# First feed-forward matrix by halves of its input for two blocks at once, two modulation groups wholly on VectorE

## The chip, the core and the metric

The kernel runs on one core of a Trainium2 chip. The metric is the device time of one execution in microseconds (us). Short names: PE is TensorE's matrix multiplication, PEld its weight loads, DVE is VectorE, ACT is ScalarE, POOL is GpSimd, SP is SyncE, whose queue issues most of the loads.

## The reference, cut to what matters

One encoder layer over 256 tokens of width 2048: windowed attention, then a squared-ReLU feed-forward part of width 8192, each between a modulation by the condition c and a layer norm.

```python
c_act = silu(c)
sh_m, sc_m, g_m, sh_f, sc_f, g_f = split(c_act @ mod_w + mod_b, 6)   # mod_w: 2048 x 12288
y = windowed_gqa_sink(x * (1 + sc_m) + sh_m, ...)                    # 32 heads, 8 key heads
x = layer_norm(ALPHA * x + (1 + g_m) * y, ln_mix_g, ln_mix_b)
hff = x * (1 + sc_f) + sh_f                                          # 256 x 2048
u = square(relu(hff @ w1 + b1))                                      # w1: 2048 x 8192
y = u @ w2 + b2                                                      # w2: 8192 x 2048
x = layer_norm(ALPHA * x + (1 + g_f) * y, ln_mlp_g, ln_mlp_b)
```

## The kernel before

**Arithmetic.** Every large product is made of three: each operand is split into a high part (rounded to the 32-bit matmul format) and a low part (the rest), and high x high, high x low and low x high are summed in PSUM. The high part of a weight piece is cast on ACT (line 218, `wh`), the low part subtracted on DVE (line 190, `wl`).

**The stream.** All weights come in pieces of 1 MB (128 x 2048) through one ordered list, `S.q`, filled by `S.plan` before any work is emitted. Five raw buffers (`RAWS`) take the loads from SP's queue, in the order of the list. `pump` walks along the list: a weight piece gets its two casts and its two low parts when there is room (five half pieces of each kind); a *modulation step* (a piece with a `use`) is carried out there and then, at most two for each call. `S.main()` hands out the next weight piece, `S.done()` returns half of it and pumps. At `S.stop`, the end of the attention part, the walk halts until the feed-forward part begins; `S.vecs(4)` then carries out the four steps that are planned behind it.

**Modulation.** `Mod` computes c_act @ (columns of mod_w). `m_mix` and `m_ff` are scale and shift of the two parts in groups of columns; a group of `m_ff` belongs to 4 of the 16 input tiles of hff and has 8 steps, 2 input tiles each. A step listed in the group's `dve` is two accumulating instructions of 128 x 1024 on DVE (lines 304 and 306), any other is 8 narrow matmuls on PE (line 274), which the profile records as 16. If a group has DVE steps, a closing matmul quad (8 records) adds the accumulator's rows up. `ff_columns(g)` then turns the result into per-input scale and bias by transposes (line 326) and small DVE work; `ff_input(g)` transposes four tiles of the normed rows `xs` (line 834), applies scale and bias, and splits the result (lines 840 to 848) into `h2[g]`. `m_gm` and `m_gf` are the gates, 16 steps each; `m_gf` is wholly on DVE.

**Attention slots.** Slots n = -2 to 20 interleave the score, softmax and value work of 16 head groups with late `wqkv` pieces and, from n = 5, the 16 pieces of `wo` (`project`). `SLOT_FILL` says how many modulation steps are planned ahead of each slot's piece: 34 in all, that is `m_gm`, groups 0 and 1 of `m_ff` and two steps of group 2; four more stand behind the stop. Slots 3 and 4 have no weight piece. In the last call of `project` the residual is added, the statistics are taken (`add_gated`, `norm_scalars`, lines 688 to 704) and the first quarter of `xs` is normed (`normed`, lines 717 and 719).

**Feed-forward.** Four blocks of 16 hidden tiles of 128. Block 0's first matrix goes by halves of the input: `W1A` lists the pieces `w1a[kg, fq]` (4 input tiles x 4 hidden tiles), first for input tiles 0 to 7 (kg 0 and 1) and then for 8 to 15; three 256-wide matmuls for each pair of tiles (lines 904 to 906). After the first half ACT copies the sums into `uacc` (line 910), after the second DVE adds them (line 912), and `square_split` makes the hidden rows. `W1_FILL` plans the remaining steps of groups 2 and 3 between the pieces. Blocks 1 to 3 use `ff_hidden`: pieces `w1b`, one hidden tile and all 16 input tiles each, with a 512-wide and a 256-wide matmul for each pair (lines 928 and 929). `ff_out` is the second matrix, 16 pieces a block (lines 439 to 441). The steps of `m_gf` lie beside block 1. `xs` stays in its four buffers from the first norm to the end; in block 1 it is prepared for the last residual (lines 973 and 974). All 128 x 1024 work tiles come from one pool of 26 buffers (`g4`).

**Order.** The text of the program gives the priority of an instruction on its engine; the tile framework places one that it reckons ready ahead of earlier ones that are not, and adds the waits.

Of the kernel before, what the change touches and what calls it, by code (L numbers as in the profile page):

```python
# [11 lines left out]
F32 = mybir.dt.float32  # L12
# [8 lines left out]
S = 256  # L21
# [20 lines left out]
def hybrid_kernel(ctx: ExitStack, tc: tile.TileContext, a, out: bass.AP):  # L42
# [6 lines left out]
    gen = ctx.enter_context(tc.tile_pool(name="gen", bufs=26))  # L49
    psa = ctx.enter_context(tc.tile_pool(name="psa", bufs=5, space=PSUM))  # L50
# [310 lines left out]
    m_ff = groups(a["modf"], FFG, [(1, 5, 7), (1, 4, 5, 6), (2,), (1, 2, 4, 5, 6, 7)])  # L361
# [30 lines left out]
    late = [m_gm] + [m[0] for m in m_ff[:3]]  # L392
# [9 lines left out]
    W1_FILL = [1, 1, 1, 0, 0, 2, 0, 3, 0, 0, 0, 0, 0, 0, 0, 0]  # L402
    SLOT_FILL = dict(enumerate([0, 1, 2, 1, 0, 1, 3, 0, 1, 3, 2, 0, 3, 5, 1, 1, 3, 2, 1, 3, 0, 0, 1], -2))
# [9 lines left out]
    W1A = [(kg, fq) for p in ((0, 1), (2, 3)) for q in ((0, 1), (2, 3)) for kg in p for fq in q]  # L413
    for n, (kg, fq) in enumerate(W1A):
        left = [m.n - m.planned for m, _, _ in m_ff]
        for _ in range(max(W1_FILL[n], left[2] if n == 6 else 0, left[2] + left[3] if n == 8 else 0)):
            m_ff[2 if m_ff[2][0].planned < m_ff[2][0].n else 3][0].plan()
        S.plan(a["w1a"][kg, fq])
    NF = FF // 128 // BLK
    for blk in range(BLK):  # L420
        for f in range(NF):
            if blk:
                if blk == 1 and f % 2:
                    m_gf.plan()
                S.plan(a["w1b"][(blk - 1) * NF + f])
        for c in range(4):
            for kg in range(4):
                if blk == 1 and kg % 2:
                    m_gf.plan()
                S.plan(a["w2"][blk, c, kg], None, blk == BLK - 1 and c == 3 and kg > 1)  # L430
# [423 lines left out]

    h2 = [ff_input(0)]
    for c in range(1, 4):
        for t in range(NT):
            normed(c, t)

# [25 lines left out]
    uacc = [g4() for _ in range(4)]  # L885
    us = []
    opened = {}
    for n, (kg, fq) in enumerate(W1A):
        if n in (1, 7, 9):
            ff_columns(len(h2))  # L890
            h2.append(ff_input(len(h2)))
        wh, wl = S.main()
        for fp in range(2):
            if kg % 2 == 0:
                opened[fq, fp] = psa.tile([128, 512], F32, name="pa")
# [61 lines left out]
    for blk in range(BLK - 1):  # L957
        if blk:
            us = ff_hidden(blk)
# [133 lines left out]
```

## Time and profile before

| | |
|---|---|
| median of 3 runs | 1133.12 us (1132.92 to 1133.7) |
| profiled execution | 1131.72 us |
| span of its instructions | 1130.0 us |
| mean granted PE clock | 0.994 |
| moved | 288.50 MB, mean 255 GB/s |

The attention part lasts until about 388.6 us of the span, the feed-forward part from there to 1117.4, and the last norm and stores follow. In rows of groups, "busy" is the union of a group's durations and the last number is the idle time of the engine ahead of them; matmuls are pipelined, so the time of one in a sequence is read from start to start, not from its length.

### The profile page before, as it was taken

The numbers are of one execution on the slowest core, as the hardware profiler recorded it, in microseconds if no ns is written. First come the engines' busy times: TensorE is split into PE (matmuls) and PEld (weight loads), VectorE is DVE, ScalarE is ACT, GpSimd is POOL, SyncE is SP. The second block draws the span as 40 slices with busy tenths as digits, with TensorE's granted clock in tenths as the row PEclk, the third lists the DMA queues.
The fourth block names the chain that finished last, engine by engine and source line by source line (L and its number), as shares of the span: only waits on it lengthen the run. The fifth ranks groups of instructions, "written<-read, shape, count | busy, mean of one in ns | idle before, by whom it ended". The sixth has DMA issues, their size and how long they took to land.

```text
span 1130.0 us, 15722 instructions
## 1 busy us (share of the span) xinstructions
PE 1091.6 (97%) x6224; PEld 876.6 (78%) x6224; DVE 810.1 (72%) x1123; ACT 539.3 (48%) x841; POOL 28.9 (3%) x47
## 2 busy tenths in 40 slices
PE   4899999999999999999999999999999999999995
PEld 2566677666676799998888888888888888888884
DVE  5556878987989977865568887966665656665576
ACT  2242345786676264753344543335454334444340
POOL 2000000000000000000000001020000000000001
PEclk9999999999999999999999999999999999999998
DMA  9998988876886599655577788775555557555522
GB/s 349 389 381 327 362 318 324 311 258 250 314 319 234 222 377 368 229 185 194 202 278 282 271 284 306 288 258 204 186 187 190 195 202 269 187 187 186 186 75 75
DMA packets 43866, 288.50 MB, mean 255 GB/s; under 512 B 5232, under 2 KB 7440, under 8 KB 10000
## 3 DMA queue, kind: packets, MB, share of 16 engines
q1 hardware_dynamic: 40640, 279.82, 67.5%
q0 software_dynamic: 2304, 6.36, 1.8%
q10 hardware_dynamic: 848, 1.31, 0.3%
q8 instruction: 49, 0.80, 0.3%
q14 instruction: 25, 0.20, 0.0%
HBM read 285.37 MB, written 2.10 MB: 254 GB/s over the span
## 4 chain that ended last, share of the span: by engine, by line
PE 91%; DVE 4%; DMA 3%; ACT 1%; issue 1%; DVEq 0%; ACTq 0%
PE pa L440 16%; PE pa L441 16%; PE pa L439 16%; PE pa L928 16%; PE pa L929 8%; PE pm L274 4%; PE pa L905 3%; PE pa L904 3%; PE pa L906 3%; DMA raw<-in_wqkv 2%; PE pa L680 2%; PE pt L665 1%; DVE wl L190 1%; PE pa L626 1%; PE pt L594 1%; DVE g L306 1%
## 5 line engine op out<-in xcount | busy, mean ns | idle before, releaser
L190 DVE TENSOR_TENSOR wl<-raw,wh 128x1024 fp32r<-128x1024 f32 x332 | 405.6, 1228 | 219.4 <-ACT wh L218 218.8
L218 ACT CAST wh<-raw 128x1024 fp32r<-128x1024 f32 x332 | 347.7, 1053 | 441.9 <-PE pa L441 232.9
L439 PE MATMUL pa<-wh,g 128*128 128x512 f32 x816 | 322.7, 397 | 4.0 <-ACT wh L218 4.0
L440 PE MATMUL pa<-wl,g 128*128 128x512 f32 x816 | 321.2, 394 | 2.8 <-DVE wl L190 2.8
L441 PE MATMUL pa<-wh,g 128*128 128x512 f32 x816 | 320.4, 393 | 0.0
L928 PE MATMUL pa<-g,wh 128*128 128x512 f32 x768 | 270.1, 396 | 0.0
L929 PE MATMUL pa<-g,wl 128*128 128x256 f32 x768 | 215.5, 281 | 0.0
L439 PEld LDWEIGHTS pa<-wh,g 128*128 128x128 f32 x816 | 153.6, 189 | 45.0 <-issue 6.5
L440 PEld LDWEIGHTS pa<-wl,g 128*128 128x128 f32 x816 | 154.2, 189 | 37.3 <-DVE wl L190 4.4
L441 PEld LDWEIGHTS pa<-wh,g 128*128 128x128 f32 x816 | 154.0, 189 | 35.7 <-issue 3.5
L928 PEld LDWEIGHTS pa<-g,wh 128*128 128x128 f32 x768 | 144.1, 188 | 34.6
L929 PEld LDWEIGHTS pa<-g,wl 128*128 128x128 f32 x768 | 145.1, 189 | 0.2
L306 DVE SCALAR_TENSOR_TENSOR g<-raw,cact,g 128x1024 f32<-128x1024 f32 (+1 forms) x83 | 100.6, 1216 | 9.4 <-DMA raw<-in_modgf 6.2
L905 PE MATMUL pa<-g,wh 128*128 128x256 f32 x256 | 72.7, 285 | 0.4 <-DVE g L848 0.4
L904 PE MATMUL pa<-g,wh 128*128 128x256 f32 x256 | 72.5, 286 | 0.0
L906 PE MATMUL pa<-g,wl 128*128 128x256 f32 x256 | 72.3, 283 | 0.0
L274 PE MATMUL pm<-raw,cact 128*32 128x256 f32 (+2 forms) x800 | 59.2, 406 | 8.9 <-DMA raw<-in_modm 7.9
L904 PEld LDWEIGHTS pa<-g,wh 128*128 128x128 f32 x256 | 48.8, 192 | 1.3 <-issue 0.8
L905 PEld LDWEIGHTS pa<-g,wh 128*128 128x128 f32 x256 | 49.1, 192 | 0.9 <-DVE g L848 0.8
L512 DVE TENSOR_TENSOR g<-g,pa 128x512 f32<-128x512 f32 x44 | 29.8, 682 | 27.0 <-PE pa L441 27.0
L906 PEld LDWEIGHTS pa<-g,wl 128*128 128x128 f32 x256 | 49.1, 192 | 0.0
L274 PEld LDWEIGHTS pm<-raw,cact 128*32 128x32 f32 x800 | 22.6, 114 | 32.7 <-issue 13.8
(169 smaller groups left out, 801.7 us busy)
## 6 DMA issues: line engine op xcount, KB each, us to landing
raw<-in_w SPq DMA_DIRECT2D x64, 1024.0 KB, 5.0
raw<-in_w1b SPq DMA_DIRECT2D x48, 1024.0 KB, 4.9
raw<-in_modm SPq DMA_DIRECT2D x32, 1024.0 KB, 8.1
raw<-in_modf SPq DMA_DIRECT2D x32, 1024.0 KB, 7.1
raw<-in_wqkv SPq DMA_DIRECT2D x24, 1024.0 KB, 7.1
raw<-in_modgm SPq DMA_DIRECT2D x16, 1024.0 KB, 5.3
raw<-in_wo SPq DMA_DIRECT2D x16, 1024.0 KB, 6.9
raw<-in_w1a SPq DMA_DIRECT2D x16, 1024.0 KB, 8.1
```

What stands on the lines that cost most here:

```text
L190: nc.vector.tensor_sub(l, r, f32(self.hs[n]))
L218: nc.scalar.copy(h, s)
L274: nc.tensor.matmul(self.ps[32 * j:32 * j + 32, :w], lhsT, rhs[j], start=self.first, stop=stop)
L306: nc.vector.scalar_tensor_tensor(p[:, :e], s, cact[:, kt:kt + 1], p[:, :e], op0=OP.mult, op1=OP.add)
L439: nc.tensor.matmul(ps, xh, wh, start=start, stop=False)
L440: nc.tensor.matmul(ps, xh, wl, start=False, stop=False)
L441: nc.tensor.matmul(ps, xl, wh, start=False, stop=stop)
L904: nc.tensor.matmul(o, wh(w, 128), hh, start=new, stop=False)
L905: nc.tensor.matmul(o, wh(w, 128), hl, start=False, stop=False)
L906: nc.tensor.matmul(o, wl(w, 128), hh, start=False, stop=end)
L928: nc.tensor.matmul(ps, wh(k, 128), hb, start=k == 0, stop=False)
L929: nc.tensor.matmul(ps[:, :256], wl(k, 128), hb[:, :256], start=False, stop=k == NK - 1)
```

## The change

The first matrix of blocks 0 and 1 is computed together for the first half of the input: `w1a` now holds 32 pieces (8 columns `fq` of 4 hidden tiles), and pass 0 is kg 0 and 1 for all eight columns, 16 pieces. The second half follows for block 0 (8 pieces), then block 0's `ff_out`, then the second half for block 1 and its `ff_out`. Blocks 2 and 3 keep `ff_hidden`, from 32 pieces `w1b`. So `uacc` has eight buffers.

Groups 2 and 3 of `m_ff` are put wholly on DVE (8 steps each), and all 16 steps are planned in pass 0, two ahead of its first piece and one ahead of each of the next 14; `ff_columns` and `ff_input` of groups 1, 2 and 3 come at pieces 1, 8 and 15. The slots get 28 steps, spread evenly, and the four behind the stop are the last of group 1 (three on DVE, one on PE). The steps of `m_gf` lie beside the `ff_out` of blocks 0 and 1.

`xs` is written to a DRAM tile by POOL's queue as each quarter is normed, and read back into new buffers at block 2, where it is prepared for the last residual. The bias b2 is loaded by quarters of its row into small buffers in place of two large ones.

```diff
@@ -47,6 +47,7 @@
+    far = ctx.enter_context(tc.tile_pool(name="far", bufs=1, space=bass.MemoryType.DRAM))
@@ -358,7 +359,7 @@
-    m_ff = groups(a["modf"], FFG, [(1, 5, 7), (1, 4, 5, 6), (2,), (1, 2, 4, 5, 6, 7)])
+    m_ff = groups(a["modf"], FFG, [(1, 5, 7), (1, 4, 5, 6), range(8), range(8)])
@@ -389,7 +390,7 @@
-    late = [m_gm] + [m[0] for m in m_ff[:3]]
+    late = [m_gm] + [m[0] for m in m_ff[:2]]
@@ -399,8 +400,7 @@
-    W1_FILL = [1, 1, 1, 0, 0, 2, 0, 3, 0, 0, 0, 0, 0, 0, 0, 0]
-    SLOT_FILL = dict(enumerate([0, 1, 2, 1, 0, 1, 3, 0, 1, 3, 2, 0, 3, 5, 1, 1, 3, 2, 1, 3, 0, 0, 1], -2))
+    SLOT_FILL = dict(enumerate([0, 1, 1, 1, 1, 1, 2, 1, 1, 2, 1, 1, 2, 2, 1, 1, 2, 1, 1, 2, 1, 1, 1], -2))
@@ -410,24 +410,37 @@
-    W1A = [(kg, fq) for p in ((0, 1), (2, 3)) for q in ((0, 1), (2, 3)) for kg in p for fq in q]
-    for n, (kg, fq) in enumerate(W1A):
-        left = [m.n - m.planned for m, _, _ in m_ff]
-        for _ in range(max(W1_FILL[n], left[2] if n == 6 else 0, left[2] + left[3] if n == 8 else 0)):
-            m_ff[2 if m_ff[2][0].planned < m_ff[2][0].n else 3][0].plan()
-        S.plan(a["w1a"][kg, fq])
     NF = FF // 128 // BLK
-    for blk in range(BLK):
-        for f in range(NF):
-            if blk:
-                if blk == 1 and f % 2:
-                    m_gf.plan()
-                S.plan(a["w1b"][(blk - 1) * NF + f])
-        for c in range(4):
-            for kg in range(4):
-                if blk == 1 and kg % 2:
-                    m_gf.plan()
-                S.plan(a["w2"][blk, c, kg], None, blk == BLK - 1 and c == 3 and kg > 1)
+    W1P = [[(kg, fq) for q in qs for kg in p for fq in (q, q + 1)]
+           for p, qs in [((0, 1), (0, 2, 4, 6)), ((2, 3), (0, 2)), ((2, 3), (4, 6))]]
+    W1_FILL = [2, 1, 1, 1, 1, 1, 1, 1, 1, 1, 1, 1, 1, 1, 1, 0]
+    def plan_ff():
+        def first(p):
+            for n, (kg, fq) in enumerate(W1P[p]):
+                for _ in range(0 if p else W1_FILL[n]):
+                    m_ff[2 if m_ff[2][0].planned < m_ff[2][0].n else 3][0].plan()
+                S.plan(a["w1a"][kg, fq])
+        def second(blk):
+            for c in range(4):
+                for kg in range(4):
+                    if blk < 2 and kg % 2:
+                        m_gf.plan()
+                    S.plan(a["w2"][blk, c, kg], None, blk == BLK - 1 and c == 3 and kg > 1)
+        first(0)
+        for blk in range(BLK):
+            if blk < 2:
+                first(1 + blk)
+            else:
+                for f in range(NF):
+                    S.plan(a["w1b"][(blk - 2) * NF + f])
+            second(blk)
+    plan_ff()
@@ -852,10 +865,17 @@
+    z_far = far.tile([128, 4096], F32, name="z_far")
+    def spill(c):
+        nc.gpsimd.dma_start(z_far[:, c * 1024:c * 1024 + 1024], xs[c])
     h2 = [ff_input(0)]
+    spill(0)
 ...
+        spill(c)
@@ -882,37 +902,41 @@
-    uacc = [g4() for _ in range(4)]
-    us = []
-    opened = {}
-    for n, (kg, fq) in enumerate(W1A):
-        if n in (1, 7, 9):
-            ff_columns(len(h2))
-            h2.append(ff_input(len(h2)))
-        wh, wl = S.main()
 ...
-            S.done()
-            av = uacc[fq][:, fp * 512:fp * 512 + 512]
-            if kg == 1:
-                nc.scalar.copy(av, ps)
-            elif kg == 3:
-                nc.vector.tensor_add(av, av, ps)
-                u = g4(F32R)
-                square_split(av, fq * 4 + fp * 2, 2, u, 0)
-                us.append(u)
+    uacc, opened = {}, {}
+    def ff_first(p):
+        us = []
+        for n, (kg, fq) in enumerate(W1P[p]):
+            if p == 0 and n in (1, 8, 15):
+                ff_columns(len(h2))
+                h2.append(ff_input(len(h2)))
+            wh, wl = S.main()
+            if kg == 0:
+                uacc[fq] = g4()
+            for fp in range(2):
+                if kg % 2 == 0:
+                    opened[fq, fp] = psa.tile([128, 512], F32, name="pa")
+                ps = opened[fq, fp]
+                for fi in range(2):
+                    o = ps[:, fi * 256:fi * 256 + 256]
+                    for k in range(4):
+                        w = (fp * 2 + fi) * 4 + k
+                        hb = ff_in(4 * kg + k)
+                        hh, hl = hb[:, :256], hb[:, 256:]
+                        new, end = kg % 2 == 0 and fi + k == 0, kg % 2 == 1 and fi == 1 and k == 3
+                        nc.tensor.matmul(o, wh(w, 128), hh, start=new, stop=False)
+                        nc.tensor.matmul(o, wh(w, 128), hl, start=False, stop=False)
+                        nc.tensor.matmul(o, wl(w, 128), hh, start=False, stop=end)
+                S.done()
+                av = uacc[fq][:, fp * 512:fp * 512 + 512]
+                if kg == 1:
+                    nc.scalar.copy(av, ps)
+                elif kg == 3:
+                    nc.vector.tensor_add(av, av, ps)
+                    u = g4(F32R)
+                    square_split(av, fq * 4 + fp * 2, 2, u, 0)
+                    us.append(u)
+        return us
@@ -952,22 +976,26 @@
+    ff_first(0)
     ys = [g4() for _ in range(4)]
-    bf = bias_all(a["b2"])
     for blk in range(BLK - 1):
-        if blk:
-            us = ff_hidden(blk)
+        us = ff_hidden(blk) if blk == 2 else ff_first(1 + blk)
+        if blk == 2:
+            xs = [g4() for _ in range(4)]
+            for c in range(4):
+                nc.gpsimd.dma_start(xs[c], z_far[:, c * 1024:c * 1024 + 1024])
         for c in range(4):
-            if blk == 1:
-                gb = [sml.tile([128, 512], F32, name="gb", tag="t2", bufs=4) for _ in range(2)]
-                for n in range(2):
-                    nc.gpsimd.dma_start(gb[n], a["lnrow"][n:n + 1, c * 512:c * 512 + 512].partition_broadcast(128))
+            if blk != 1:
+                gb = [sml.tile([128, 512], F32, name="gb", tag="t2", bufs=4) for _ in range(2 if blk else 1)]
+                for n, b in enumerate(gb):
+                    row = a["lnrow"][n:n + 1] if blk else a["b2"]
+                    nc.gpsimd.dma_start(b, row[:, c * 512:c * 512 + 512].partition_broadcast(128))
             for t, ps in enumerate(ff_out(blk, us, c)):
                 if blk == 0:
-                    nc.vector.tensor_add(part(ys, t, c), ps, bf(c))
+                    nc.vector.tensor_add(part(ys, t, c), ps, gb[0])
                 else:
                     nc.vector.tensor_add(part(ys, t, c), part(ys, t, c), ps)
-            if blk == 1:
+            if blk == 2:
@@ -1059,9 +1087,9 @@
-    n0 = FF // BLK
-    wa = w1[:, :n0].reshape(4, 4, 128, 4, 4, 128)
-    o["w1a"] = cc(wa.transpose(0, 3, 2, 4, 1, 5).reshape(4, 4, 128, 2048))
+    n0 = FF // 2
+    wa = w1[:, :n0].reshape(4, 4, 128, 8, 4, 128)
+    o["w1a"] = cc(wa.transpose(0, 3, 2, 4, 1, 5).reshape(4, 8, 128, 2048))
```

In `ff_first` the matmuls between `S.main()` and `S.done()` are those of the old loop, unchanged; block 2's residual preparation is the old block 1's.

14 lines of the change are left out of this document (removed).

## The prediction

> **What bounds the kernel now.** I read the page first, then one windows answer by stage, then the timelines of TensorE (PE) and VectorE (DVE) around the start of the feed-forward part.
>
> ```profile
> PE 1091.6 (97%) x6224; PEld 876.6 (78%) x6224; DVE 810.1 (72%) x1123; ACT 539.3 (48%) x841; POOL 28.9 (3%) x47
> PE 91%; DVE 4%; DMA 3%; ACT 1%; issue 1%; DVEq 0%; ACTq 0%
> ```
>
> The first line is busy time over the span, the second the chain that ended last: nine tenths of it lie on PE. Time is won only by taking work off PE, as long as nothing else makes PE wait. By stage (us, then busy time of PE, PEld, DVE, ACT, POOL, then PEclk, DMA share, GB/s):
>
> ```profile
> 184.00:388.57 204.57, 204.26 (x1206) 143.40 (x1202) 176.26 (x296) 139.91 (x330) 1.12 (x2) 1.00 0.74 274
> 388.57:396.64 8.07, 7.09 (x98) 3.50 (x96) 6.97 (x29) 2.71 (x6) 0.00 (x0) 1.00 0.85 310
> 396.64:457.16 60.52, 60.13 (x515) 57.46 (x512) 47.76 (x70) 35.36 (x53) 0.53 (x1) 1.00 0.93 361
> 457.16:496.64 39.48, 39.48 (x331) 39.48 (x330) 30.47 (x39) 24.91 (x39) 0.53 (x1) 1.00 0.60 211
> 583.60:674.00 90.40, 90.40 (x514) 78.39 (x513) 74.14 (x95) 44.50 (x62) 0.54 (x1) 1.00 0.77 275
> ```
>
> The rows are the attention slots, the turn from attention to feed-forward, the first feed-forward matrix of block 0 (two rows) and that of block 1. PE is full everywhere but in the turn. DVE is 86% busy in the slots (176.26 of 204.57) and 79% in the first 60 us of block 0. The turn, on PE:
>
> ```profile
> 388.72 3.66 PE L274 MATMUL pm<-raw,cact 128*32 128x256 f32 x64
> 393.36 1.05 PE L274 MATMUL pm<-raw,cact 128*32 128x256 f32 x10 [0.98 <-DMA raw<-in_modf]
> 395.27 0.88 PE L834 MATMUL pt<-ident,g 128*128 128x128 f32 x6
> 396.64 0.51 PE L904 MATMUL pa<-g,wh 128*128 128x256 f32 x2
> 397.52 0.39 PE L905 MATMUL pa<-g,wh 128*128 128x256 f32 x1 [0.37 <-DVE g L848]
> ```
>
> and on DVE:
>
> ```profile
> 387.29 1.21 DVE L190 TENSOR_TENSOR wl<-raw,wh 128x1024 fp32r<-128x1024 f32 x1
> 391.89 0.26 DVE L694 BATCH_NORM_AGGREGATE mv<-st 128x2 f32<-128x24 f32 x1
> 393.97 1.46 DVE L719 TENSOR_SCALAR g<-g,mv,r 128x512 f32<-128x512 f32 x3
> 396.46 0.54 DVE L846 TENSOR_SCALAR g<-pt,a,b 128x256 f32<-128x256 f32 x1 [1.04 <-ACT g L840]
> 397.04 0.42 DVE L848 TENSOR_TENSOR g<-g,g 128x256 fp32r<-128x256 f32 x1
> ```
>
> The 8.07 us of the turn are set by the statistics on DVE and the transposes behind them. The modulation matmuls (L274) there, 74 records in the first two rows, ride in a wait. Also, the first low halves of w1a (L190 at 387.29) are ready before the turn, so DVE can give it wholly to the normalisation.
>
> **Part 1: modulation steps leave PE.** Group 2 of m_ff goes from 7 PE steps to none, group 3 from 2 to none: 9 steps of 16 records. Price of one, among slot matmuls:
>
> ```profile
> 288.32 0.39 PE L441 MATMUL pa<-wh,g 128*128 128x512 f32 x1
> 288.63 1.07 PE L274 MATMUL pm<-raw,cact 128*32 128x256 f32 x16
> 289.63 0.50 PE L440 MATMUL pa<-wl,g 128*128 128x512 f32 x1
> 289.97 0.40 PE L441 MATMUL pa<-wh,g 128*128 128x512 f32 x1
> ```
>
> From 288.32 to 289.97 are 1.65 us; two plain matmuls take 0.23 us each (0.39 long, pipelined), so the step costs 1.2 us. Of the 9, four to five lie in the turn and come to nothing: they filled a wait. By the plan's counts, steps 0 and 1 of group 2 lie in the slots, one more was drawn forward into them, and the two of group 3 lie beside block 0. So 3 steps leave the slots, -3.6 us, and with them the closing quad of group 1 (8 records, about half a step, 0.7 us) moves into the turn: -4.3. Against it: one of three m_gm steps in slot n=4, which has no weight matmuls of its own, is now planned later:
>
> ```profile
> 237.66 1.06 PE L274 MATMUL pm<-raw,cact 128*32 128x512 f32 x8
> ```
>
> Where it filled a wait there, 1.0 us comes back (0 if that slot was full): slots **-3.3**, between -4.3 and -3.3. Beside block 0, two steps go (-2.4) and the closing quad of group 2 comes in from the turn (+0.7): **-1.7**. The turn itself cannot shrink below the DVE chain.
>
> **Part 2: block 1 in the form of block 0.** A block's 1 MB pieces now take three 256-wide matmuls where L928 and L929 took a 512-wide and a 256-wide one. Rows of the two pure stretches (457.16 to 496.64, and block 1):
>
> ```profile
> L905 PE MATMUL pa<-g,wh 128*128 128x256 f32 x109 | 30.8, 283 | 0.0
> L928 PE MATMUL pa<-g,wh 128*128 128x512 f32 x256 | 90.5, 399 | 0.0
> ```
>
> Three times 109 matmuls in 39.48 us are 120.7 ns each; a block has 768, so 92.7 us. L928's 256 pairs took 90.40. **+2.3** us. The accumulators' copies (ACT) and adds (DVE) lie in stages where both are under 80% busy: nothing, and some 1 us if a bank were freed late.
>
> **Part 3: VectorE in the turn.** Eighteen more accumulating steps of 128x1024 come onto DVE (group 2: from 2 to 16, group 3: from 12 to 16), and three of group 1 (two instructions each) move from the slots to behind the stop of the stream, ahead of group 2's first two steps, which now stand ahead of the first w1a load. Prices:
>
> ```profile
> 428.49 5.24 DVE L306 SCALAR_TENSOR_TENSOR g<-raw,cact,g 128x1024 f32<-128x1024 f32 x4
> 433.65 2.36 DVE L190 TENSOR_TENSOR wl<-raw,wh 128x1024 fp32r<-128x1024 f32 x2
> L848 DVE TENSOR_TENSOR g<-g,g 128x256 fp32r<-128x256 f32 x13 | 5.4, 421 | 0.2
> L846 DVE TENSOR_SCALAR g<-pt,a,b 128x256 f32<-128x256 f32 x7 | 3.8, 540 | 1.6 <-ACT g L840 1.6
> ```
>
> 1.31 us an accumulation, 1.18 a low half, 2 x 0.54 + 4 x 0.42 = 2.8 for the DVE share of one ff_input. Work behind the stop is drawn forward where DVE is free:
>
> ```profile
> 362.30 0.75 DVE L304 TENSOR_SCALAR g<-raw,cact 128x1024 f32<-128x1024 f32 x1
> 367.70 1.28 DVE L306 SCALAR_TENSOR_TENSOR g<-raw,cact,g 128x1024 f32<-128x1024 f32 x1
> 350.00:388.57 38.57, 38.57 (x186) 29.35 (x184) 35.66 (x53) 16.49 (x28) 0.00 (x0) 1.00 0.53 194
> ```
>
> The two first rows are such a step of group 2, twenty us ahead of the turn. Room before the turn is 2.9 us idle, these 2.0, and 2.4 if w1a's first low halves wait: 7.3 us for group 1's 6 x 1.31 = 7.9. So about one instruction, and all of group 2's start and w1a's first low halves, fall behind the statistics. From 393.97 DVE then has 1.5 (normed), 1.3 (left over), 2.8 (first input), 4 x 1.31 = 5.2, 2 x 1.18 = 2.4: 13.2 us, first piece ready at 407.2. Next 2.6 + 2.4: 412.2. Then 2.8 + 0.5 for input group 1 and 5.0: 420.5 for the third piece. PE meanwhile runs all matmuls that need no low half, 64 for two pieces, but closes the third piece 1.0 us behind its last low half, at 421.5, where unhindered it would be there at 396.64 + 0.37 + 3 x 5.79 + 2.1 (transposes and quads) = 416.5. Later pieces cost DVE 5.0 us against PE's 5.8, so the lateness stays as it is: 5.0, or 3.7 without the left-over instruction. I take **+4.0**. Ends: 0, if these accumulations fit in earlier gaps as the two rows above did; 3.7 + 6 x 1.31 = +11.6, if all six are left.
>
> What is queued behind these accumulations on DVE are the low halves, and PE waits for those. On SP's queue the first w1a load stood behind five modulation loads and now stands behind six:
>
> ```profile
> 378.26 0.33 SPq L182 DMA_DIRECT2D raw<-in_w1a  x1
> ```
>
> One load more is some 2.6 us at 400 GB/s (windows under B), so it lands by 386: ahead of DVE's turn to it, no cost of its own. Spills and reloads (POOL's queue, 4 x 512 KB each way) delay no engine: xs is read last by ff_input(3), and reloaded a block ahead of its use. Nearest row of such a transfer:
>
> ```profile
> g<-in_lnrow POOLq DMA_DIRECT2D x4, 512.0 KB, 5.7
> ```
>
> 5.7 us stand against 20 us of ff_out before the first use; without that cover 5.7 us would be lost. The four b2 pieces, 256 KB each in place of two of 512, have the same cover. Half of m_gf's steps move beside block 0's ff_out, and the residual's preparation from block 1's to block 2's:
>
> ```profile
> 496.64:583.60 86.96, 86.96 (x385) 71.99 (x385) 49.56 (x49) 35.51 (x36) 0.00 (x0) 1.00 0.62 215
> ```
>
> Eight steps of two accumulations are 21 us, so 70.5 of 87 us on DVE: no cost; had DVE been full, the 21 us would be.
>
> **Part 4: the rest of pass 0.** 16 pieces bring DVE 32 x 1.31 + 32 x 1.18 + 4 x 2.8 + 4 = 95 us, beside PE's 100.0 - 1.7 = 98.3: 97% full. Before, the same stretch and the 39.48 us behind it are 100.0 us for 92.7 of matmuls, 2.4 of two steps, 0.7 of a quad and about 4.4 of three inputs' transposes (eight at the 0.15 us of the L834 row, and 0.3): at 79% PE lost nothing that could be seen. Between nothing and what the full DVE costs the first pieces (4.0) I take **+1.0**, nearer to the row at 79%, because the pieces' five buffers give two pieces' lead.
>
> **Part 5: the clock.** With the turn's filling gone PE idles some 5 us in it. What idling does here, early in the run:
>
> ```profile
> 38.70 0.73 PE L439 MATMUL pa<-wh,g 128*128 128x512 f32 x2 [2.85 <-ACT wh L218]
> 40.32 0.63 PE L441 MATMUL pa<-wh,g 128*128 128x512 f32 x1
> 40.75 0.63 PE L439 MATMUL pa<-wh,g 128*128 128x512 f32 x1
> 40.00:43.30 3.30, 3.30 (x9) 2.57 (x9) 3.26 (x3) 0.00 (x0) 0.00 (x0) 0.54 0.91 318
> ```
>
> After 2.85 us idle the granted clock was 0.54 for 3.3 us, a matmul every 0.43 us in place of 0.23: eight of them, 1.6 us lost. Half of it would lie under waits for DVE: **+0.8**, 0 to 1.6. The Trainium skill (TensorE: Matmul & The Clock Gate, the HAM clock gate) says the clock halves after an idle window of about 3.4 us and returns after a busy one as long; by it the loss is an estimated 1.7 us, and the row agrees in kind, though 2.85 us sufficed.
>
> **Sum.** -3.3 - 1.7 + 2.3 + 4.0 + 1.0 + 0.8 = +3.1. The profiled execution took 1131.72 (span 1130.0), so 1134.8 for such a one; the median, 1133.12, lies 1.4 above it: **1136.2**.
>
> **Rivals.** (A) DVE keeps up: accumulations fit in earlier gaps, the clock stays. Then -4.3 - 1.7 + 2.3 = -3.7: 1129.4. For it: the step at 362.30, and PE's freedom to run matmuls without low halves first. Against: only 7.3 us of room. It decides if all low halves of the first three pieces are there by 416. (B) Pass 0 is bound by DVE or by the loads throughout: Part 3 at its end, +11.6, Part 4 at 4, the clock at 1.6: -2.7 + 17.2 = +14.5 at most; taken half way from the forecast, +8.8, 1141.9. It decides where pieces take over 6.1 us on PE. For the loads:
>
> ```profile
> 396.64:406.00 9.36, 8.97 (x78) 7.56 (x75) 7.74 (x16) 7.82 (x13) 0.00 (x0) 1.00 1.02 425
> 406.00:416.00 10.00, 10.00 (x86) 10.00 (x85) 7.87 (x11) 6.89 (x11) 0.00 (x0) 1.00 0.98 397
> ```
>
> Two loads, 2.1 MB, in 6.1 us are 344 GB/s, and the spill adds 2.1 MB; 397 to 425 were reached. The Trainium skill (DMA: Bandwidth & Descriptors, Specifications) gives some 358 GB/s as a core's share of memory; by it the first eight pieces with the spill, 18.9 MB, would take an estimated 53 us against PE's 49, some 4 us slower. The rows exceed that figure, so I give this little weight. (C) The slots' steps filled waits too, so the change takes nothing off the chain there: +3.1 + 3.3 = +6.4, 1139.5. Against: PE was 204.26 of 204.57 busy.
>
> **How the numbers follow.** Forecast 0.45, A 0.30, B 0.17, C 0.08. A measurement can tell about 0.2% (2.3 us) from no change. The forecast's own range (DVE 0 to 7) is 1132 to 1139: of its 0.45, 0.17 within 2.3 us and 0.28 slower; A 0.27 faster and 0.03 within; B and C slower. Faster 0.27, same 0.20, slower 0.53. The range takes in A's value and B's middle: 1129 to 1142.
>
> **What would show it.** Right: a PE wait of 3 to 6 us in all, between the first L904-form matmul and the third piece, released by L190; clock under 1 behind the turn; fewer L274 records in the slots, which end 3 us sooner; block 1's first matrix at 92 to 93 us. Wrong: the third piece done 20 us behind the first matmul (A); PE waits for L190 past the sixth piece, or for raw (B); slots as long as before (C).

## The result, and the profile after

The changed kernel takes **1151.25 us** (median of four runs, 1149.58 to 1153.07) against 1133.41 for the kernel before beside it: a ratio of 1.0149, 95% interval 1.0136 to 1.0163. Forecast were 1136.2, range 1129 to 1142. The direction was right; the loss was 17.8 us and not 3.1.

The profiled execution took 1153.07 us. Its page, busy time and chain:

```profile
span 1151.4 us, 15997 instructions
PE 1092.5 (95%) x6336; PEld 890.1 (77%) x6336; DVE 828.9 (72%) x1117; ACT 543.4 (47%) x841; POOL 35.2 (3%) x57
PE 87%; DVE 7%; DMA 3%; ACT 1%; issue 1%; DVEq 0%; ACTq 0%
```

PE has as much work as before (1092.5 us against 1091.6) in a span 21.4 us longer (of the two profiled executions; the medians lie 17.8 us apart). DVE's share of the chain rises from 4 to 7 per cent. By stage, in windows with the same columns as in the prediction:

```profile
184.00:388.17 204.17, 201.49 (x1146) 141.07 (x1145) 168.80 (x290) 137.99 (x327) 1.11 (x2) 0.99 0.67 247
388.17:399.32 11.15, 4.53 (x36) 2.05 (x33) 11.13 (x33) 4.80 (x9) 0.89 (x2) 0.65 0.68 240
399.32:514.70 115.38, 103.13 (x816) 100.45 (x817) 89.70 (x109) 55.37 (x77) 1.73 (x3) 0.92 0.87 323
399.32:426.43 27.11, 15.64 (x107) 14.77 (x107) 22.64 (x30) 10.11 (x15) 1.73 (x3) 0.75 0.95 361
426.43:467.80 41.37, 40.59 (x318) 39.51 (x319) 32.81 (x39) 20.17 (x27) 0.00 (x0) 0.93 0.94 345
467.80:514.40 46.60, 46.60 (x392) 45.87 (x391) 34.11 (x43) 25.06 (x35) 0.00 (x0) 1.00 0.77 284
514.40:560.60 46.20, 46.20 (x387) 46.20 (x386) 32.35 (x38) 25.97 (x37) 0.00 (x0) 1.00 0.58 205
647.70:693.80 46.10, 46.10 (x386) 46.10 (x385) 34.61 (x39) 25.66 (x36) 0.00 (x0) 1.00 0.59 206
```

In this order: the slots; the turn; pass 0 (its 768 weight matmuls, as many as block 0's first matrix had before); then three parts of pass 0; the second halves of blocks 0 and 1.

| stage (profiled, us) | before | after | difference | forecast |
|---|---|---|---|---|
| slots, to the last `project` matmul | 204.57 | 204.17 | -0.4 | -3.3 |
| turn, to the first weight matmul | 8.07 | 11.15 | +3.1 | 0 |
| first 768 weight matmuls | 100.0 | 115.4 | +15.4 | +4.1 |
| block 1's first matrix (both second halves after) | 90.6 | 92.3 | +1.7 | +2.3 |
| block 2's first matrix | 91.8 | 93.3 | +1.5 | 0 |

The 115.4 us are lost early: from 399.32 to 426.43 PE is busy 15.64 of 27.11 us, while from 467.80 on nothing is lost, with DVE at 73%. Three waits, 11.5 us together, carry most of it (timeline of PE: start, length, group, then the idle time ahead and what ended it):

```profile
401.55 0.58 PE L928 MATMUL pa<-g,wh 128*128 128x256 f32 x1 [1.43 <-DVE g L861]
420.86 1.09 PE L847 MATMUL pt<-ident,g 128*128 128x128 f32 x4 [5.56 <-DVE shf L333]
426.43 1.52 PE L927 MATMUL pa<-g,wh 128*128 128x256 f32 x5 [4.48 <-ACT g L853]
```

The two long ones are input group 1, which the third piece is the first to need: its transposes wait for `ff_columns` (L333), its first matmul for the scaled input (L853). Why these were late stands in the queue of SP, in one row of PE, in ACT's timeline and in DVE's:

```profile
362.82 19.25 SPq L183 DMA_DIRECT2D raw<-in_modf  x5
389.45 0.33 SPq L183 DMA_DIRECT2D raw<-in_w1a  x1
396.29 0.33 SPq L183 DMA_DIRECT2D raw<-in_w1a  x1
404.05 0.33 SPq L183 DMA_DIRECT2D raw<-in_w1a  x1
```

```profile
388.32 1.07 PE L275 MATMUL pm<-raw,cact 128*32 128x256 f32 x16
```

```profile
394.39 1.99 ACT L219 CAST wh<-raw 128x1024 fp32r<-128x1024 f32 x2 [1.46 <-DMA raw<-in_w1a]
413.49 1.99 ACT L219 CAST wh<-raw 128x1024 fp32r<-128x1024 f32 x2 [8.66 <-DMA raw<-in_w1a]
425.81 0.56 ACT L853 ACTIVATE g<-pt,b,a 128x256 fp32r<-128x256 f32 x1 [5.22 <-DVE b L834]
```

```profile
391.29 1.27 DVE L307 SCALAR_TENSOR_TENSOR g<-raw,cact,g 128x1024 f32<-128x1024 f32 x1
392.88 1.28 DVE L307 SCALAR_TENSOR_TENSOR g<-raw,cact,g 128x1024 f32<-128x1024 f32 x1
394.99 1.27 DVE L307 SCALAR_TENSOR_TENSOR g<-raw,cact,g 128x1024 f32<-128x1024 f32 x1
...
414.57 1.23 DVE L191 TENSOR_TENSOR wl<-raw,wh 128x1024 fp32r<-128x1024 f32 x1 [4.35 <-ACT wh L219]
415.71 1.28 DVE L307 SCALAR_TENSOR_TENSOR g<-raw,cact,g 128x1024 f32<-128x1024 f32 x1
...
419.24 0.15 DVE L333 TENSOR_TENSOR scf<-pt,pack 128x4 f32<-128x4 f32 x1
419.36 1.28 DVE L307 SCALAR_TENSOR_TENSOR g<-raw,cact,g 128x1024 f32<-128x1024 f32 x1
...
424.42 1.28 DVE L307 SCALAR_TENSOR_TENSOR g<-raw,cact,g 128x1024 f32<-128x1024 f32 x1
425.62 0.15 DVE L834 TENSOR_TENSOR b<-b,shf 128x4 f32<-128x4 f32 x1
```

Six modulation pieces stand ahead of the first w1a piece: group 1's last four (the first of them loaded at 359.31, ahead of the row of five) and group 2's first two. Group 2's two are loaded at 378.15 and 381.75, into the raw buffers that come free then. Then all five buffers hold modulation pieces, four for DVE and one for PE. The next one comes free when PE has done its one step (L275, until 389.39, behind the last matmul of `project`), so the first w1a load is issued at 389.45, 11.2 us later than the 378.26 of before. The next two w1a loads, at 396.29 and 404.05, each follow the end of an accumulation, and the third piece lands at 413.4, where it landed at 402.2 before. Three accumulations (391.29 to 394.99) stand between the statistics of the last norm, which makes the turn longer. DVE even idles 4.35 us ahead of 414.57 for want of the third piece. Then the chain of six small instructions that ends in `b` (L834) takes from 419.24 to 425.62, since four accumulations of 1.28 us and a low half stand between its members.

### The profile page after: what moved, and what is told of

It reads as the page before. It is cut to its first block, busy times and chain, and to the rows that moved or that the text cites. A ratio compares the mean times of both kernels' runs of the same rounds, so it can differ in the third digit from the quotient of the medians.

```text
span 1151.4 us, 15997 instructions
## 1 busy us (share of the span) xinstructions
PE 1092.5 (95%) x6336; PEld 890.1 (77%) x6336; DVE 828.9 (72%) x1117; ACT 543.4 (47%) x841; POOL 35.2 (3%) x57
## 4 chain that ended last, share of the span: by engine, by line
PE 87%; DVE 7%; DMA 3%; ACT 1%; issue 1%; DVEq 0%; ACTq 0%
PE pa L453 16%; PE pa L454 16%; PE pa L452 16%; PE pa L952 10%; PE pa L953 5%; PE pa L928 5%; PE pa L929 5%; PE pa L927 5%; PE pm L275 4%; DMA raw<-in_wqkv 2%; DVE g L307 2%; PE pa L693 2%; DVE wl L191 1%; PE pt L678 1%; DMA raw<-in_w1a 1%
## 5 line engine op out<-in xcount | busy, mean ns | idle before, releaser
L453 PE MATMUL pa<-wl,g 128*128 128x512 f32 x816 | 321.2, 394 | 2.8 <-DVE wl L191 2.8
L453 PEld LDWEIGHTS pa<-wl,g 128*128 128x128 f32 x816 | 154.0, 189 | 37.5 <-DVE wl L191 4.4
L952 PE MATMUL pa<-g,wh 128*128 128x512 f32 x512 | 181.0, 399 | 0.0
L927 PE MATMUL pa<-g,wh 128*128 128x256 f32 x512 | 146.5, 288 | 4.5 <-ACT g L853 4.5
L928 PE MATMUL pa<-g,wh 128*128 128x256 f32 x512 | 146.9, 287 | 2.2 <-DVE g L861 2.2
L307 DVE SCALAR_TENSOR_TENSOR g<-raw,cact,g 128x1024 f32<-128x1024 f32 (+1 forms) x101 | 125.4, 1248 | 17.2 <-DMA raw<-in_modgf 16.4
L952 PEld LDWEIGHTS pa<-g,wh 128*128 128x128 f32 x512 | 96.2, 188 | 24.0
L927 PEld LDWEIGHTS pa<-g,wh 128*128 128x128 f32 x512 | 99.9, 196 | 5.3 <-ACT g L853 5.3
L928 PEld LDWEIGHTS pa<-g,wh 128*128 128x128 f32 x512 | 99.9, 195 | 3.3 <-DVE g L861 2.8
L275 PE MATMUL pm<-raw,cact 128*32 128x256 f32 (+2 forms) x656 | 49.2, 417 | 8.0 <-DMA raw<-in_modm 8.0
L275 PEld LDWEIGHTS pm<-raw,cact 128*32 128x32 f32 x656 | 18.2, 117 | 28.8 <-issue 14.9
```

The lines of the kernel that those rows point to most:

```text
L275: nc.tensor.matmul(self.ps[32 * j:32 * j + 32, :w], lhsT, rhs[j], start=self.first, stop=stop)
L307: nc.vector.scalar_tensor_tensor(p[:, :e], s, cact[:, kt:kt + 1], p[:, :e], op0=OP.mult, op1=OP.add)
L453: nc.tensor.matmul(ps, xh, wl, start=False, stop=False)
L927: nc.tensor.matmul(o, wh(w, 128), hh, start=new, stop=False)
L928: nc.tensor.matmul(o, wh(w, 128), hl, start=False, stop=False)
L952: nc.tensor.matmul(ps, wh(k, 128), hb, start=k == 0, stop=False)
```

## The experiments

The expectations name theories by letter. S (the spill) and V (DVE's total work) are told where they come up; two run through all of them. **L, the line**: modulation pieces for DVE ahead of the weight pieces hold the raw buffers, and their accumulations stand ahead of what PE waits for. **C, the clock**: the emptied turn halves PE's clock, and that makes the loss. Ratios are to the kernel before, run beside each, with 95% intervals.

**struct.** The halves, the spill and the reload stay; which modulation steps are on PE and where they are planned goes back.

```diff
-groups(a["modf"], FFG, [(1,5,7), (1,4,5,6), range(8), range(8)]);  late: m_ff[:2]
+groups(a["modf"], FFG, [(1,5,7), (1,4,5,6), (2,), (1,2,4,5,6,7)]);  late: m_ff[:3]
+SLOT_FILL as before;  W1_FILL = [1,1,1,0,0,2,0,3,2,0,...]
```

> The halves for two blocks, the spill and the reload stay; the modulation goes back to what it was before (groups 2 and 3 partly on PE, the old fill of the slots, two steps of group 2 and all of group 3 beside pass 0). Theory L, that the loss comes from the line of modulation pieces held for VectorE ahead of the first weight pieces: the turn is 8 us again, no wait of over 1 us behind it, and only the form of block 1 is paid, +2.3 us against the kernel before: 1135 to 1137. Rival S, that the spill or the two-block form itself starves pass 0: 1145 to 1151, with the waits of the changed kernel still there.

Measured 1135.92, ratio 1.0016 [1.0004, 1.0028]. The turn and the first 768 matmuls are as before:

```profile
389.89:397.96 8.07, 7.10 (x100) 3.50 (x97) 6.99 (x29) 2.71 (x6) 1.08 (x2) 1.00 0.83 302
397.96:498.21 100.25, 99.86 (x843) 96.99 (x841) 67.11 (x88) 54.70 (x77) 1.07 (x2) 1.00 0.80 312
```

So the halves for two blocks, the trip through DRAM and the rest of the new order cost 2 us, and some 16 of the 17.8 come from the modulation.

**fill_late.** The 16 steps of groups 2 and 3 stand ahead of pieces 4 to 15, and inputs 2 and 3 come later.

```diff
-W1_FILL = [2,1,1,1,1,1,1,1,1,1,1,1,1,1,1,0];  inputs at n in (1, 8, 15)
+W1_FILL = [0,0,0,0,2,1,1,1,1,1,1,1,1,2,2,2];  inputs at (p, n) in ((0,1), (0,12), (1,1))
```

> The changed kernel, with the first step of group 2 planned ahead of the fifth piece instead of two ahead of the first, and the inputs of group 2 and 3 made at piece 12 and beside block 0's second half. Theory L: the first weight load stands behind four modulation loads instead of six and the next three behind none, so the 11 us wait ahead of input group 1 goes for the most part: 10 to 14 us faster than the changed kernel, 1137 to 1141; the turn stays long, since group 1's three VectorE steps are still in it. Rival V, that VectorE's total work in pass 0 is the bound (97% full): the wait only moves behind the fifth piece, 1147 to 1152.

Measured 1139.99, ratio 1.0051 [1.0035, 1.0067]: 11.3 us of the loss were the line's place (its loads and its accumulations together, with inputs 2 and 3 moved along). The first two w1a loads go out ahead of the turn, at 377.55 and 381.14, and the 768 matmuls take 103.11 us. The first row merges these two with the loads at 388.85 and 391.98:

```profile
377.55 14.76 SPq L183 DMA_DIRECT2D raw<-in_w1a  x4
```

```profile
387.57:398.72 11.15, 4.53 (x35) 2.05 (x33) 11.13 (x33) 5.87 (x10) 0.89 (x2) 0.76 0.70 241
398.72:501.83 103.11, 100.52 (x812) 98.50 (x813) 87.02 (x104) 49.72 (x68) 1.25 (x3) 0.96 0.93 353
```

**g1_slots.** Group 1 is done in the slots, by the older uneven counts, 32 in all; nothing is left for behind the stop. The line stays early.

```diff
-SLOT_FILL [0,1,1,1,1,1,2,1,1,2,1,1,2,2,1,1,2,1,1,2,1,1,1]
+SLOT_FILL [0,1,2,1,0,1,3,0,1,3,2,0,3,5,1,1,3,2,1,2,0,0,0]
```

> The changed kernel, with group 1 finished in the slots by the old fill cut at 32 steps; group 2's first two steps follow the stop at once. Theory L: two modulation loads instead of six stand ahead of the first weight piece, none of the accumulations sits between the statistics, slot 4 has its third step again: turn 8 to 9 us, waits behind it under 4 us, slots 2 to 3 us shorter: 1134 to 1139. Rival C, that the idle clock alone makes the loss (PE still has nothing to do in the turn): the clock still falls to 0.5 behind it, 1143 to 1149. Rival V: 1147 to 1152.

Measured 1144.42, ratio 1.0084 [1.0059, 1.0109]: 6.8 us less than the change. The slots end at 385.24, 3.3 us sooner than before, which is the saving that the prediction reckoned and the even counts lost. The rest missed theory L: the turn is no shorter (11.65 us), since an accumulation of group 2 (388.78) and a low half (390.55) now stand between the statistics, and behind it PE still waits 3.04 us for a weight piece. The time lies in rival C's span and the clock is at 0.50 behind the turn, so this run doesn't tell the two apart.

**spill_late.** The spill stands at pieces 9 to 12 in the text of the program.

```diff
-    spill(0)  # behind ff_input(0), and spill(c) behind each normed(c, t)
+    if p == 0 and n in (9, 10, 11, 12): spill(n - 9)
```

> The changed kernel, with the four spills issued at pieces 9 to 12 of pass 0 instead of at its start. Theory L: the third weight load lands some 3 us sooner (9.4 us from issue to landing before, 6 to 7 here), and nothing else changes: 1148 to 1151. Rival S, that the spill's 2.1 MB starve the first pieces: the wait ahead of input group 1 goes, 1138 to 1144.

Measured 1152.38, ratio 1.0158 [1.0133, 1.0183], and the edit did not take effect: the framework issued the four transfers at 397.87 to 400.13 us as before, since they were ready. The spill had to be tried otherwise (no_spill, below).

**pe4.** The four steps behind the stop go on PE.

```diff
-(1, 4, 5, 6)   # group 1
+(0, 1, 2, 3)
```

> The changed kernel, with group 1's steps 0 to 3 on VectorE and its last four, those behind the stop, on PE. The turn then has PE work again and no accumulation of group 1 among the statistics, but the first weight piece still stands behind six modulation pieces, the last two of them for VectorE. Theory L: the turn is back at 8 to 9 us and the clock stays up in it, yet the waits behind it stay, 6 to 12 us: 1141 to 1147. Rival C, that the halved clock makes the loss: no wait of over 1 us, 1134 to 1139.

Measured 1154.07, ratio 1.0179 [1.0161, 1.0197], above both spans. The filling did not fall into the turn: all four steps were placed ahead of the last ten matmuls of `project` (L453 and on), where they delay the statistics: the slots end at 394.04, 5.9 us later than in the change.

```profile
387.47 3.44 PE L275 MATMUL pm<-raw,cact 128*32 128x256 f32 x59
...
391.48 0.50 PE L453 MATMUL pa<-wl,g 128*128 128x512 f32 x1
```

The turn is 8.17 us and the 768 matmuls still take 113.9, with waits of 4.24 and 3.23 us for input group 1: the waits stay without accumulations among the statistics, as theory L had it. The clock fell behind this turn too, so C is not excluded by it.

**both.** fill_late and g1_slots together.

> Late start of groups 2 and 3 and group 1 finished in the slots, together: no modulation piece between the stop and the first weight pieces, no accumulation in the turn, but PE idle in it. Theory L: no wait of over 1.5 us behind the turn. Against the kernel before +2.3 (block 1's form), -1.7 (two steps beside block 0), -3.6 (three steps from the slots), +1.6 (clock): 1130 to 1134. Rival C: the clock falls for two windows of 4 us or more and the turn is 11 us as in the two single edits: 1136 to 1140.

Measured 1136.29, ratio 1.0022 [1.0010, 1.0034]: 15.0 of the 17.8 us gone, but 2 us above theory L's span. Time and turn are those of rival C; both_gate, below, tells what made the turn long. The 768 matmuls are at 100.9 us, but the turn stays at 11.28:

```profile
386.39:397.67 11.28, 2.45 (x10) 1.43 (x9) 9.65 (x32) 5.46 (x9) 1.28 (x3) 0.65 0.60 204
```

Low halves of w1a, now loaded early, have taken the place of the accumulations between the statistics:

```profile
389.62 1.22 DVE L191 TENSOR_TENSOR wl<-raw,wh 128x1024 fp32r<-128x1024 f32 x1
390.76 0.15 DVE L713 RECIPROCAL r<-sd 128x1 f32<-128x1 f32 x1
...
391.33 1.22 DVE L191 TENSOR_TENSOR wl<-raw,wh 128x1024 fp32r<-128x1024 f32 x1
392.46 0.15 DVE L717 TENSOR_TENSOR r<-r,qq 128x1 f32<-128x1 f32 x1
```

**both_warm.** both with 36 short matmuls of no use ahead of `ff_columns(0)`, to keep the clock up.

> The kernel of both edits with 36 narrow matmuls (72 records, 4.5 us) on idle data put into the turn, their result unused: they change nothing but PE's idling. If the clock costs what its rows say, the granted clock stays at 1.0 behind the turn and the time is 1.5 to 3 us under that of both edits; if the clock's loss lies under waits for VectorE, within 1 us of it; if the fillers themselves are in the way of the transposes, 1 us or more over it.

Measured 1137.08, ratio 1.0033 [1.0022, 1.0043]: no gain. But the fillers did not keep the clock up. They ran at once, from 387.67 to 391.76, PE then idled 3.23 and 2.39 us ahead of the transposes, and in the first 4 us of pass 0 the granted clock was 0.56 (0.50 in both):

```profile
399.75:403.75 4.00, 4.00 (x19) 3.89 (x20) 2.51 (x8) 3.64 (x7) 0.60 (x2) 0.56 0.94 369
```

Pass 0 is 0.9 us shorter (100.07), the turn 0.7 longer (12.01), and the slots end 1.4 later. So this run doesn't show what a clock at full speed behind the turn would be worth; theory C is decided by both_gate.

**late_pe4.** fill_late, a slot list of 28 and the four steps behind the stop on PE.

> Late start of groups 2 and 3, three steps again in slot 4, and group 1's last four steps, behind the stop, on PE, its first four on VectorE. By the ledger of PE the turn is filled by steps that cost nothing there: seven steps of 1.2 us and a quad leave the slots (-9.1), -1.7 beside block 0, +2.3 for block 1: 1124 to 1128, the fastest of all. Rival: VectorE holds the slots, with three steps of group 1 more in them (86% busy before): 1130 to 1135.

Measured 1142.75, ratio 1.0088 [1.0063, 1.0114], far above both spans. The PE steps were again drawn ahead of the end of `project`, and five low halves and the casts stood among the statistics: a turn of 16.25 us.

```profile
388.97:405.22 16.25, 2.23 (x9) 1.44 (x9) 11.72 (x28) 9.35 (x13) 1.29 (x3) 0.61 0.93 373
```

**both_gate.** both, with the first eight low halves tied to the end of the statistics.

```diff
+one = tensor_scalar(rstd of the second half, * 0.0 + 1.0)
-nc.vector.tensor_sub(l, r, f32(h))
+nc.vector.scalar_tensor_tensor(l, r, one, f32(h), op0=mult, op1=subtract)   # first eight
```

> The kernel both with one edit: the first eight low halves of w1a take a factor of one that is computed from the second half's norm scale, so that none of them can stand among the statistics on VectorE. Theory (the turn of 11.3 us in both is made by the low halves between the statistics): the turn goes to 8.1 to 9 us, and the time to 1133 to 1134.5, if pass 0 keeps its 100.6 us; up to 1 us is given back where the first piece's low half is then late. Rival (the turn is longer because nothing fills it and the clock halves, not because of the order on VectorE): the turn stays over 10.5 us and the time at 1135.5 to 1137.

Measured 1132.54, ratio 0.9993 [0.9983, 1.0004], 3.7 us below both. The turn is 7.81 us though nothing fills it and the clock is 0.72 in it: its length is the order on DVE. Behind it the clock is at 0.50, as in both (last row, the first 4 us of pass 0), and the time is still no longer than before: theory C falls as the main cause.

```profile
385.02:392.83 7.81, 2.45 (x11) 1.43 (x8) 7.70 (x27) 4.51 (x8) 1.07 (x2) 0.72 0.03 13
392.83:494.57 101.74, 99.76 (x812) 97.77 (x813) 86.75 (x104) 49.52 (x68) 1.06 (x2) 0.97 0.93 352
392.83:396.83 4.00, 3.06 (x13) 2.77 (x13) 3.81 (x8) 3.64 (x7) 1.06 (x2) 0.50 0.97 260
```

By the profiles the turn is 3.5 us shorter, the slots end 1.4 sooner and pass 0 takes 0.8 back; another 1.4 us is block 2's first matrix, whose code the edit doesn't touch (last section).

**before_m3.** The kernel before, with one edit.

```diff
-(2,), (1, 2, 4, 5, 6, 7)]
+(2,), range(8)]
```

> The kernel before with one edit: group 3 of m_ff wholly on VectorE (its two steps on TensorE become four accumulations of 1.3 us). The halves stay block 0's alone, nothing is spilled. Theory L (accumulations on VectorE cost nothing as long as no weight piece and no input waits behind them; these four stand at pieces 6 to 8, where VectorE was at 79 per cent): two steps of 1.2 us leave TensorE, 1130.5 to 1131.5. Rival (VectorE's line at pieces 6 to 8 is already full, since all of group 2's and 3's steps stand in the first eight pieces): input group 2 or 3 comes late and the time is 1133 to 1136, with a wait of TensorE near 430 to 440 us.

Measured 1131.88, ratio 0.9990 [0.9981, 0.9999]; the 768 matmuls take 98.76 us in place of 100.0. Two more steps on DVE gain a little if they stand where DVE has room, without any halves. This kernel also has the longer of block 2's two times (last section). With the shorter one, 1.4 us less, it would be an estimated 1130.5 us, as fast as the fastest version below.

**mix.** The late line, the older slot counts, and group 2 divided between PE and DVE.

```diff
-(1, 4, 5, 6), range(8), range(8)];  late: m_ff[:2]
+(1, 4, 5, 6), (4, 5, 6, 7), range(8)];  late: m_ff[:3];  SLOT_FILL as in g1_slots
+W1_FILL = [0,0,0,0,1,1,1,1,1,1,1,1,1,1,1,1];  inputs at ((0,1), (0,11), (1,1))
```

> The changed kernel with the late line of fill_late and the even older slot counts of g1_slots (32 steps, group 1 done in the slots), and group 2 divided: steps 0 to 3 on TensorE behind the stop, where the kernel before had four as well, steps 4 to 7 and all of group 3 on VectorE, one ahead of each of pieces 4 to 15. Theory L: the turn is filled with the four TensorE steps again and takes 8 to 9 us, the first w1a load stands behind modulation pieces that TensorE frees at once, pass 0 takes 98 to 101 us, the slots 2 to 3 us less than before: 1130 to 1133. Rival (the framework draws the four TensorE steps ahead of the last ten matmuls of project, as in late_pe4, and low halves get among the statistics): slots as long as before and a turn of 11 us or more, 1135 to 1140.

Measured 1133.41, ratio 0.9995 [0.9986, 1.0004]: the turn 9.36 us, pass 0 98.95, PE's four steps inside the turn.

**mix_gate.** mix with the factor of both_gate.

> The kernel mix with both_gate's factor of one on the first eight low halves of w1a. mix took 9.36 us in the turn (1.22 us of a low half between the two halves' scales, at 388.26 us, is in its statistics) and 98.95 us for pass 0; both_gate 7.81 and 101.74. If the two gains add, the turn goes to 7.8 to 8.3 us, pass 0 stays at 99 to 100, and the time is 1131.5 to 1132.7, which would beat the kernel before by 1 to 2 us. Rival (the low halves that are held back come late for the first pieces, which in mix are already behind the statistics): pass 0 takes 100.5 us or more, and the time stays at 1133 to 1134.

Measured **1130.49**, ratio 0.9971 [0.9958, 0.9984], the fastest version of all. Turn and pass 0 came as expected, but the gains hardly add: by the profiles the turn is 1.9 us shorter than in mix, while slots and pass 0 are 0.7 longer each, and 1.4 us come from block 2's first matrix, which the expectation did not count. That the time fell below the expected span is luck to that extent.

```profile
184.00:386.15 202.15, 201.83 (x1178) 142.84 (x1177) 174.95 (x296) 139.91 (x330) 1.12 (x2) 1.00 0.72 264
386.15:393.61 7.46, 5.36 (x74) 2.96 (x72) 7.36 (x27) 3.34 (x7) 0.80 (x2) 0.95 0.71 262
393.61:493.28 99.67, 98.97 (x806) 97.25 (x807) 78.00 (x89) 52.73 (x71) 1.34 (x3) 0.97 0.91 350
```

**no_spill.** The changed kernel without the spill; the reload reads a weight instead, so the last residual is left out.

```diff
-nc.gpsimd.dma_start(z_far[:, c * 1024:c * 1024 + 1024], xs[c])
-nc.gpsimd.dma_start(xs[c], z_far[:, c * 1024:c * 1024 + 1024])
+nc.gpsimd.dma_start(xs[c], a["w2"][0, c, 0][:, :1024])
```

> The changed kernel without the four spill transfers (2.1 MB); the reload in block 2 reads as many bytes of a weight instead, so the last residual is not the reference's. Theory L (the line of modulation pieces and VectorE's accumulations make the loss): the third w1a load lands some 4 us sooner, at 409 us in place of 413.4, but input group 1's scale waits for the accumulations all the same, and the time falls by 0 to 3 us, to 1148 to 1151. Rival (the spill's traffic is what makes the third weight piece late, and everything behind it): it falls by 5 us or more, to 1146 or below, and the waits of 5.6 and 4.5 us near 415 to 426 us shrink by half.

Measured 1148.72, ratio 1.0127 [1.0107, 1.0146], 2.5 us below the change and inside theory L's span. The two ratios' intervals overlap, but the traces give the spill a price: pass 0 is 111.62 us in place of 115.38. Without the spill's 2.1 MB the third w1a load lands at 408.55 in place of 413.41, and the wait of 5.56 us is 1.02; the one behind it stays, being the accumulations':

```profile
416.07 0.63 PE L847 MATMUL pt<-ident,g 128*128 128x128 f32 x4 [1.02 <-DVE shf L333]
421.92 1.52 PE L927 MATMUL pa<-g,wh 128*128 128x256 f32 x5 [5.22 <-ACT g L853]
```

Windows over the same stretch, after and then without the spill, show it in the last two columns (DMA share, GB/s):

```profile
398.00:414.00 16.00, 14.56 (x99) 13.86 (x99) 12.10 (x15) 7.32 (x12) 2.61 (x4) 0.78 0.99 378
```

```profile
398.00:414.00 16.00, 14.55 (x100) 13.86 (x99) 15.89 (x19) 8.46 (x13) 0.00 (x0) 0.78 0.83 301
```

**mix_gate_sl.** mix_gate, each spill held back behind a small write of a late sum to the same place.

```diff
+if p == 0 and n in (12, 13, 14, 15):
+    c = n - 12
+    nc.gpsimd.dma_start(z_far[:, c * 1024:c * 1024 + 1], uacc[5][:, 0:1])
+    spill(c)
```

> The kernel mix_gate with each spill transfer held back until a sum of the sixth column of hidden tiles is there (a column of it is written to the same place first), so that the spill falls at the end of pass 0, behind 460 us. Theory L (the spill costs no engine anything, the prediction's claim): the same as mix_gate, 1130 to 1131. Rival (the spill's 2.1 MB beside the first weight loads makes a wait in the first pieces): pass 0 takes 1 to 3 us less than its 99.67 and the time is 1127.5 to 1129.5. Either could lose a little if xs's buffers come free later: TensorE would then wait near the end of pass 0.

Measured 1130.99, ratio 0.9970 [0.9959, 0.9982]. The spill began at 469 us, and pass 0 took 99.75: no difference. So the spill cost time in the kernel whose weight loads were late already, and none that can be measured in the one whose loads were early.

## Why the prediction was wrong, point by point

- **Part 3, the step that failed: "it lands by 386 ... no cost of its own".** The first w1a load was priced as one load more in SP's queue, 2.6 us. But a load needs a free raw buffer, and a buffer with a modulation piece is free only once its engine has run the step. Group 2's two pieces, now for DVE and ahead of w1a, took the two buffers that came free in time; four of the five then waited for DVE and one for PE's step behind `project`. The load went out at 389.45, not at some 381, and the third landed at 413.4. fill_late, in which the two w1a loads take those places, prices the line's place at 11.3 us.
- **Part 3, "the low halves, and PE waits for those" and "the lateness stays as it is", +4.0.** The third piece's low halves were done at 418.1, even before the 420.5 of the sum. What came late was input group 1, counted as 2.8 + 0.5 us and ahead of them. Its six small instructions came behind them in a chain, with four accumulations and a low half placed between, and took 6.5 us. PE's two waits for it are 10.0 us, where 3 to 6 us for the low halves (L190) were forecast. no_spill leaves 5.22 us of the second, though its load came 4.9 us sooner.
- **Part 3, spills "delay no engine".** Wrong by some 2.5 us here (overlapping intervals, 3.8 us of pass 0 in the profiles) and right in mix_gate_sl (0.5 us, inside the intervals). The cover was the loads' lead; with the lead gone, 2.1 MB beside the third load showed. The stretch moved 378 GB/s; the Trainium skill (DMA: Bandwidth & Descriptors, Specifications) gives some 358 as a core's share, and this core alone passes it.
- **The turn "cannot shrink below the DVE chain".** Nearly true (7.46 us in mix_gate is the least), but it can grow: the prediction put "about one instruction" behind the statistics and expected none between them. Three were, 3 x 1.28 us, and the turn grew by 3.1. both_gate, which keeps DVE's large instructions out, has 7.81.
- **Slots, -3.3, measured -0.4.** 48 records of L274 did go, three steps. The term for slot n=4 was 1.0 us at most and cost about 3: weight matmuls that are 0.1 us late ahead of the slot (223.30 us) are 3.1 late behind it (251.41). PE waits 2.43 us there for ACT (L653), and the granted clock from 240.00 to 243.30 is 0.69.

```profile
240.28 0.50 PE L452 MATMUL pa<-wh,g 128*128 128x512 f32 x1 [2.43 <-ACT g L653]
```

```profile
240.00:243.30 3.30, 3.02 (x9) 1.83 (x11) 3.30 (x8) 2.20 (x9) 0.00 (x0) 0.69 0.06 7
```

  g1_slots, with the older counts, has the whole -3.3. So rival C, whose sign (slots as long as before) came, was wrong on steps in general and right on this one.
- **Part 4, "97% full".** DVE did 89.70 us in the 115.38, not 95 in 98.3, and once the line had drained PE lost nothing at 73%. +1.0 is neither shown nor needed.
- **Part 5, the clock.** It fell as forecast (0.50 from 396 to 404), and a second time that was not forecast (0.50 from 419 to 432), behind the wait for input group 1. Its price is not shown: both_warm did not keep the clock up. PE is busy 4.57 us from 399.32 to 405.32 and 5.88 from 419 to 432, so an estimate from these windows is some 5 us of pass 0 at most, part of it under waits for DVE; the range of 0 to 1.6 counted one fall alone. In slot 4 an idle time of 2.43 us was enough for a fall; the Trainium skill (TensorE: Matmul & The Clock Gate, the HAM clock gate) has an idle window of about 3.4 us, and here, as in the prediction's row, less sufficed.
- **Part 2, +2.3, measured 1.7.** The form was right: 92.3 us (46.20 and 46.10) for 768 matmuls where 92.7 were forecast; the stage before is 90.6 by its own ends.
- **Rival B** had the right side and the wrong place: bound by DVE and loads, but only until the third piece began (PE's last wait ends at 428.95), and there by the order of the line and not by rates. Its "at most +14.5" left out the buffers.

Three things stay open: how the loss divides exactly (fill_late's 11.3, g1_slots' 6.8 and no_spill's 2.5 us overlap, 15.0 for the first two together), how much of pass 0's loss is the clock, and 1.5 us of block 2, below.

## What to carry to other kernels

When a step of a shared load ring moves to another engine, price the time until its buffer is free, by that engine's place in its own work, and follow which load stands behind it; a queue's rate is only a floor. Before moving work to an engine "with room", look at where its short, chained instructions stand (statistics, scales): long ready instructions slip between them, and an order must be forced by a dependency, since a later place in the text did not do it (spill_late), while a factor computed at the end of the chain did (both_gate, 3.5 us of the turn). Spread counts evenly only where no slot lives on its filling.

## What the runs showed of the hardware

Block 2's first matrix has the same code in all these kernels and takes one of two times, with no idle time to explain it:

```profile
761.05:852.84 91.79, 91.69 (x522) 79.78 (x521) 58.86 (x83) 48.21 (x70) 0.00 (x0) 1.00 0.56 197
```

```profile
780.82:874.07 93.25, 93.14 (x522) 79.91 (x521) 58.88 (x83) 48.21 (x71) 2.70 (x5) 1.00 0.60 205
```

The first is the kernel before, with the changed kernel behind it. Behind the first three hidden tiles a tile takes 5.55 us in the one and 5.65 in the other; blocks 1 and 3 of the kernel before take 5.65 as well. The shorter time is also that of g1_slots, both_warm, late_pe4, both_gate, mix_gate and mix_gate_sl, the longer one that of struct, fill_late, spill_late, pe4, both, mix, before_m3 and no_spill (each by its one profiled execution). So 1.5 us of the result, and of both_gate's lead over both and mix_gate's over mix, hang on something that the change touches by accident; which it is was not tried.
